# Sums of activation blocks in buffers of the hidden tiles: a feed-forward with more conventional and fewer seven-product sets

## The chip, the cores and the metric

The program runs on one core of a Trainium2 chip, in one launch. The metric is the device time of that launch in microseconds (us), shown as the median of several runs with their lowest and highest. One further run was taken with the hardware profiler; every row below is from that one. Engines are called as the profile calls them: PE is TensorE, DVE is VectorE, ACT is ScalarE, SP is the engine that issues the DMAs here.

## The reference

One inference step of a small diffusion model with two layers. Each layer is a feed-forward, a mixer (attention and pooling) and a second feed-forward; the change touches only the feed-forwards, of which there are four in all. All data are fp32.

```
D_MODEL = 1024
SEQ = 128            # context tokens
DEC_SEQ = 512        # latent tokens
D_FF = ((8 * D_MODEL // 3 + 255) // 256) * 256     # 2816
...
def modulate(h, shift, scale):
    return h * (1 + scale) + shift
...
def ffn_sub(x, g, shift, scale, gate, w_in, w_out):
    h = modulate(rms_norm(x, g), shift, scale)
    a, b = jnp.split(h @ w_in, 2, axis=-1)
    return x + gate * (FFN_RESIDUAL * ((jax.nn.silu(a) * b) @ w_out))
```

The shift, scale and gate come from a product of the conditioning vector with `w_mod`; the kernel computes most of them beside the feed-forwards, as reductions on DVE.

## The kernel before

The 512 latent and 128 context tokens stand together as 640 columns, in two groups of G = 320. The activation is kept transposed: eight k-tiles of 128 rows (channels) by 640 columns. Every fp32 product is made of three fp32r matmuls: an operand is split in a high part (ACT, a copy with rounding) and a low part (DVE, the difference), and the matmuls are high by high, high by low and low by high. `split_w` (L103, L104) does that for a weight unit of 128 by 1024 and `norm_apply` (L295 to L299) for the normalised, modulated activation h; its parts are `hhi` and `hlo`.

The inner width 2816 is 22 f-tiles of 128 rows. An f-tile needs two weight units, one for a and one for b. There are two ways to make one:

- conventional (`in_one`, `start4`, the three units of `start_first`): for each of the two units, 8 k-tiles x 2 groups x 3 = 48 matmuls of 320 columns, 96 for the f-tile;
- a seven-product set (`product_set`): the 2 x 2 block products (two halves of the k-tiles by two token groups, by a and b) are made with seven block products of 4 k-tiles x 3 = 12 matmuls, 84 for the f-tile. It needs sums and differences of the weight blocks (L427 to L432, each on 128 x 512) and of the activation's four blocks h11, h12 (k-tiles 0 to 3 of groups 0 and 1), h21 and h22 (k-tiles 4 to 7).

`combine_h` makes the sums of activation blocks once in each feed-forward. For each k of 0 to 3 it recomputes h in full precision in four temporaries (`h_full`, L396 on DVE and L398 on ACT; group 1 in two pieces, of 192 and 128 columns, because the latent and the context tokens have their own modulation), takes four differences (L407 to L410), and splits each into a high part (ACT) and a low part (DVE L418): `Th`, `Tl` for T1 to T3, and for T4 the parts of h itself, k-tiles 0 to 3 of group 1, which no later product reads otherwise.

A feed-forward starts with f-tiles 0 and 1 (`start4`: four units at once, or in the first feed-forward `start_first`), makes f-tile 2 conventionally (NCONV = 3), and the other 19 as seven-product sets. `hidden` or `hidden7` make silu(a) * b, split it in `hidh`, `hidl` (a pool of 7 buffers each). The output products take the f-tiles in chunks of 6, 6, 5 and 5. `filler` puts the reductions of `w_mod` between (L157, two for each 128 x 1024 tile of it). While `start4` runs, `self.pend` applies the norm to group 1 (`norm_out`).

What sets the order: the program's calls are put on each engine by a scheduler, which can move an instruction past others on its engine; an engine then takes its instructions in the order that results. Pools set more: weight tiles as loaded have 4 buffers (`raw`, shared with the `w_mod` tiles; all loads go through SP), split weights have 5 (`whi`, `wlo`), PSUM has 8 banks. A tile waits until the earlier one in its buffer has been read for the last time.

Of the kernel before, what the change touches and what calls it, by code (L numbers as in the profile page):

```python
# [6 lines left out]
F32 = mybir.dt.float32  # L7
F32R = mybir.dt.float32r
BF16 = mybir.dt.bfloat16
AF = mybir.ActivationFunctionType  # L10
ALU = mybir.AluOpType
# [4 lines left out]
P, D, KT = 128, 1024, 8  # L16
NT, G = 640, 320
NFT = 22
CHUNKS = (6, 6, 5, 5)
NCONV = 3  # L20
EPS = 1e-6
WINDOWS = (2, 4, 8, 16)
NWM = 12
# [8 lines left out]
def grp(a, g):  # L32
    return a[:, g * G:(g + 1) * G]
# [7 lines left out]
class Body:  # L41
    def __init__(self, nc, tc, ctx, i, o):
        self.nc, self.tc, self.i, self.o = nc, tc, i, o
        self.n = 0
        self.pend, self.hold, self.chains = None, None, []
        k = self.keep = self.pool(ctx, "keep", 1)
        self.raw = self.pool(ctx, "raw", 4)
        self.wr = self.pool(ctx, "wr", 5)
        self.hp = self.pool(ctx, "hp", 1)
        self.tp = self.pool(ctx, "tp", 5)  # L50
        self.x = [k.tile([P, NT], F32, name=f"x{m}") for m in range(KT)]
        self.mod = k.tile([P, 2, 2, 9, KT], F32, name="mod")
        self.acol = k.tile([P, 2, 2, 3, KT], F32, name="acol")
        self.bmod = k.tile([P, 2, 9, KT], F32, name="bmod")
        self.gn = k.tile([P, 7, KT], F32, name="gn")
        self.cst = k.tile([P, 640], F32, name="cst")
        self.anti = self.cst[:, 512:640]
        self.ident = self.cst[:, 0:128]
        self.bones = self.cst[:, 128:256]
        self.sel = self.cst[:, 256:352]  # L60
        self.edge = self.cst[:, 352:380]
        self.ones = self.cst[:, 384:512]
# [259 lines left out]
    def norm_out(self, g, nxt):  # L322
        rstd = self.ys[g] = self.rstd(g)
        for m in range(KT):
            self.norm_one(m, g, rstd, nxt)

    def norm_one(self, m, g, rstd, nxt):
        if nxt is None:
# [58 lines left out]
        return p4  # L387


    def h_full(self, m, g, l, s):  # L390

        nc = self.nc
        t = self.g()
        x, y = grp(self.x[m], g), self.ys[g]
        for q, c in PIECES[g]:
            nc.vector.scalar_tensor_tensor(out=t[:, c], in0=x[:, c], scalar=self.acol[:, q, l, s, m:m + 1],  # L396
                                           in1=y[:, c], op0=ALU.mult, op1=ALU.mult)
            nc.scalar.activation(t[:, c], t[:, c], AF.Identity, bias=self.mod[:, q, l, 3 * s, m:m + 1])  # L398
        return t

    def combine_h(self, pool, l, s):

        nc = self.nc
        T = self.T = [[None] * 4 for _ in range(4)]
        for k in range(4):
            h11, h12, h21, h22 = (self.h_full(m, g, l, s) for m in (k, k + 4) for g in range(2))
            nc.vector.tensor_tensor(h11, h12, h11, op=ALU.subtract)  # L407
            nc.vector.tensor_tensor(h12, h22, h12, op=ALU.subtract)
            nc.vector.tensor_tensor(h22, h22, h11, op=ALU.subtract)
            nc.vector.tensor_tensor(h21, h21, h22, op=ALU.subtract)  # L410
            for j, t in enumerate((h11, h22, h12, h21)):
                if j < 3:
                    hi = pool.tile([P, G], F32R, tag=f"Th{j}{k}", name=self.nm("Th"))
                    lo = pool.tile([P, G], F32R, tag=f"Tl{j}{k}", name=self.nm("Tl"))
                else:
                    hi, lo = self.h(k, 1)
                nc.scalar.activation(hi, t, AF.Copy)
                nc.vector.tensor_tensor(lo, t, hi.bitcast(F32), op=ALU.subtract)  # L418
                T[j][k] = hi, lo

    def product_set(self, srcs):

# [11 lines left out]
        w3 = self.split_w(b)  # L434
        T1, T2, T3, T4 = self.T
        h1, h2, h3 = ([self.h(k, g) for k in r] for r, g in ((range(4), 0), (range(4, 8), 0), (range(4, 8), 1)))
# [23 lines left out]
    def ffn(self, ctx, l, j, nxt, fill=(), first=False):  # L460

        nc = self.nc
        fill = list(fill)
        spread = max(0, len(fill) - (32 if first else 28))
        if first:
            with ExitStack() as cs:
                p3 = self.start_first(self.pool(cs, "st", 1))
        hp = self.pool(ctx, "hid", 7)
        Tp = self.pool(ctx, "T", 1)
        win, wout = self.i["w_in"], self.i["w_out"]  # L470
        v = 2 + 6 * j

        def hidden(pa, pb):
            sl = self.t()
            for g in range(2):
                self.last_silu = nc.scalar.activation(grp(sl, g), pa[g][:, :G], AF.Silu)
                if self.last_rs:
                    self.after(self.last_silu, self.last_rs)
                    self.last_rs = None
                nc.vector.tensor_tensor(grp(sl, g), grp(sl, g), pb[g][:, :G], op=ALU.mult)  # L480
            return hid_split(sl)

        def hid_split(sl):
            hi = hp.tile([P, NT], F32R, tag="hidh", name=self.nm("hidh"))
            lo = hp.tile([P, NT], F32R, tag="hidl", name=self.nm("hidl"))
            nc.scalar.activation(hi, sl, AF.Copy)
            nc.vector.tensor_tensor(lo, sl, hi.bitcast(F32), op=ALU.subtract)
            return hi, lo
# [11 lines left out]
        def filler(n):  # L500
            for _ in range(n):
                if fill:
                    self.mod_tile(*fill.pop(0))

        def fill_set(f):

            if f < 7:
                filler(1)
            else:
                filler((f - 6) * spread // 15 - (f - 7) * spread // 15)  # L510

        def in_one(f, ab):
            w, p = self.unit(win[l, j, f, ab]), [self.bank() for _ in range(2)]
            for k in range(KT):
                self.mm3([p[g][:, :G] for g in range(2)], w, k, [self.h(k, g) for g in range(2)], k == 0, k == KT - 1)
            return p

        if first:
            hid = [hidden(p3[0], p3[1])]
            hid.append(hidden(p3[2], in_one(1, 1)))  # L520
        else:
            p4 = self.start4([win[l, j, f, ab] for f in range(2) for ab in range(2)])
            hid = [hidden(p4[0], p4[1]), hidden(p4[2], p4[3])]
        if fill:
            self.mod_load()
        while len(hid) < NCONV:
            pa = in_one(len(hid), 0)
            hid.append(hidden(pa, in_one(len(hid), 1)))
            if first:
                filler(4)  # L530
        self.combine_h(Tp, l, 2 * j)

        def inproj(f):
            hid.append(hidden7(*self.product_set([win[l, j, f, ab] for ab in range(2)])))
# [864 lines left out]
def layout(a):  # L1399
    import numpy as np  # L1400
    C = np.ascontiguousarray
    d = dict(consts())
    xp, xs = a["x_prompt"][0].T, a["x_sample"][0].T[:, tok()]
    d["xT"] = np.concatenate([xs, xp], 1).reshape(KT, P, NT)
# [23 lines left out]
    d["w_pool"] = a["w_pool"][0]  # L1428
    d["pscale"] = C(a["pool_scale"][0].reshape(4, P).T)
    ck = a["cache_nb_k"][0, 0].transpose(1, 2, 0)  # L1430
# [18 lines left out]
def unlay(r):  # L1449
    import numpy as np  # L1450
    y = r["yT"].reshape(D, NT)
    yp = y[:, 512:].T[None]
    ys = np.empty((512, D), y.dtype)
# [21 lines left out]
```

## Time and profile before

| | us |
|---|---|
| median of 3 runs (lowest to highest) | 2393.68 (2390.45 to 2394.62) |
| the profiled execution | 2392.37 |
| its span, first to last instruction | 2390.6 |
| PE busy | 2299.9 (96%) |
| DVE busy | 1949.5 (82%) |
| ACT busy | 1159.0 (48%) |

Busy times overlap. Matmuls are pipelined and a waiting one can still be counted as busy, so the work that PE gets done in a stretch is better read from the number of matmuls in it. [...] In a timeline the duration of an instruction overlaps the start of the next one on its engine, so the time that an instruction takes up on its engine is the distance of the starts.

### The profile page before, as it was taken

Reading aid. Unit: us, or ns where it says so; the run is one execution under the profiler, and the core shown is the slowest. Engines: PE = TensorE matmul, PEld = TensorE weight load, DVE = VectorE, ACT = ScalarE, POOL = GpSimd, SP = SyncE. Lnnn points to the kernel's source line nnn. Section 1 sums busy time; section 2 is a strip of 40 time slices with the busy share of each in tenths; the row PEclk is TensorE's granted clock in tenths of the full one; section 3 lists DMA queues with packets and bytes.
Section 4 is the critical chain, followed back from the end, with each engine's and each line's share of the span. In section 5 each row is a group of like instructions: output and inputs, shape, how many; then the busy total and the mean of one; then the engine's idle time right before and its main releaser. Section 6 shows DMA issues by size and latency. Waiting matters only on the chain.

```text
span 2390.6 us, 40708 instructions
## 1 busy us (share of the span) xinstructions
PE 2299.9 (96%) x15852; PEld 2224.0 (93%) x15852; DVE 1949.5 (82%) x3975; ACT 1159.0 (48%) x2164; POOL 2.2 (0%) x10
## 2 busy tenths in 40 slices
PE   7799999999999999999999999998999999999998
PEld 5799999998888999999989999998888898999997
DVE  6998989785889977786899898969778899565665
ACT  5534343463666534334563425347756665252443
POOL 0000000000000000000000000000000000000000
PEclk9899999999999999999989999999999999999999
DMA  7254535322111433352225353432110013222221
GB/s 288 98 177 135 176 126 180 119 97 86 55 46 46 138 129 123 113 167 75 86 71 186 112 187 124 155 105 79 36 36 28 28 54 104 88 79 84 88 67 67
DMA packets 81088, 253.38 MB, mean 106 GB/s; under 512 B 9600, under 2 KB 15360, under 8 KB 80896
## 3 DMA queue, kind: packets, MB, share of 16 engines
q1 hardware_dynamic: 80896, 250.79, 32.1%
q8 instruction: 125, 2.05, 0.3%
q14 instruction: 67, 0.55, 0.1%
HBM read 247.34 MB, written 3.41 MB: 105 GB/s over the span
## 4 chain that ended last, share of the span: by engine, by line
PE 83%; DVE 11%; ACT 3%; issue 2%; DMA 1%; DVEq 0%; ACTq 0%; SPq 0%
PE mm L124 36%; PE mm L132 13%; PE mm L133 13%; PE mm L135 13%; PE tr L618 2%; PE pv L1251 2%; DVE wlo L104 1%; PE sc L1216 1%; DVE junk L157 1%; DVE g L295 1%; DVE hlo L299 1%; DVE g L396 1%; ACT whi L103 1%; PE pv L1018 1%; PE sc L991 0%
## 5 line engine op out<-in xcount | busy, mean ns | idle before, releaser
L103 ACT ACTIVATE whi<-raw 128x1024 fp32r<-128x1024 f32 (+2 forms) x424 | 411.7, 978 | 553.2 <-PE mm L133 245.4
L104 DVE TENSOR_TENSOR wlo<-raw,whi 128x1024 fp32r<-128x1024 f32 (+2 forms) x424 | 472.1, 1118 | 110.0 <-ACT whi L103 109.6
L132 PE MATMUL mm<-hidh,whi 128*128 128x320 f32 x1408 | 427.4, 310 | 0.0
L133 PE MATMUL mm<-hidl,whi 128*128 128x320 f32 x1408 | 425.7, 308 | 0.0
L124 PE MATMUL mm<-hhi,wlo 128*128 128x320 f32 x1216 | 378.3, 311 | 5.6 <-DVE wlo L104 5.6
L124 PE MATMUL mm<-hhi,whi 128*128 128x320 f32 x1216 | 378.5, 311 | 0.8 <-ACT mm L440 0.8
L124 PE MATMUL mm<-hlo,whi 128*128 128x320 f32 x1216 | 377.5, 310 | 0.0
L135 PE MATMUL mm<-hidh,wlo 128*128 128x320 f32 x1408 | 346.1, 309 | 0.0
L157 DVE CUSTOM_DVE_ANT_0 junk<-rawm,sil 128x1024 bf16<-128x1024 f32 x256 | 311.9, 1218 | 18.1 <-DMA rawm<-in_wmT 14.5
L348 DVE SCALAR_TENSOR_TENSOR x<-mm,mod,x 128x192 f32<-128x192 f32 (+2 forms) x576 | 226.4, 433 | 111.8 <-PE mm L135 110.7
L133 PEld LDWEIGHTS mm<-hidl,whi 128*128 128x128 f32 x1408 | 264.3, 188 | 0.8
L132 PEld LDWEIGHTS mm<-hidh,whi 128*128 128x128 f32 x1408 | 264.3, 188 | 0.8
L135 PEld LDWEIGHTS mm<-hidh,wlo 128*128 128x128 f32 x1408 | 241.4, 188 | 0.0
L124 PEld LDWEIGHTS mm<-hhi,wlo 128*128 128x128 f32 x1216 | 230.6, 190 | 6.0 <-DVE wlo L104 6.0
L132 PE MATMUL mm<-hhi,whi 128*128 128x320 f32 x736 | 228.5, 324 | 7.4 <-ACT hhi L298 7.3
L124 PEld LDWEIGHTS mm<-hhi,whi 128*128 128x128 f32 x1216 | 230.7, 190 | 1.2 <-ACT mm L440 1.2
L124 PEld LDWEIGHTS mm<-hlo,whi 128*128 128x128 f32 x1216 | 230.7, 190 | 0.0
L133 PE MATMUL mm<-hlo,whi 128*128 128x320 f32 x736 | 227.1, 314 | 0.5 <-DVE hlo L299 0.2
L135 PE MATMUL mm<-hhi,wlo 128*128 128x320 f32 x736 | 211.6, 311 | 0.7 <-DVE wlo L104 0.5
L124 PE MATMUL mm<-Th,whi 128*128 128x320 f32 x608 | 192.9, 317 | 8.4 <-ACT whi L103 5.1
L124 PE MATMUL mm<-Tl,whi 128*128 128x320 f32 x608 | 191.2, 314 | 0.0
L124 PE MATMUL mm<-Th,wlo 128*128 128x320 f32 x608 | 190.8, 314 | 0.4 <-DVE wlo L104 0.4
(212 smaller groups left out, 4144.8 us busy)
## 6 DMA issues: line engine op xcount, KB each, us to landing
raw<-in_w_in SPq DMA_DIRECT2D x176, 512.0 KB, 3.5
rawm<-in_wmT SPq DMA_DIRECT2D x128, 512.0 KB, 3.5
raw<-in_w_out SPq DMA_DIRECT2D x64, 384.0 KB, 3.6
raw<-in_w_out SPq DMA_DIRECT2D x64, 320.0 KB, 2.9
wm<-in_wm SPq DMA_DIRECT2D x16, 512.0 KB, 10.2
raw<-in_w_ab SPq DMA_DIRECT2D x12, 512.0 KB, 4.3
raw<-in_w_c SPq DMA_DIRECT2D x10, 512.0 KB, 3.5
sil<-in_c SPq DMA_DIRECT2D x8, 512.0 KB, 5.3
```

What stands on the lines that cost most here:

```text
L103: a = (nc.scalar.activation(hi[:, :n], r[:, :n], AF.Copy), nc.vector.tensor_tensor(lo[:, :n], r[:, :n], hi[:, :n].bitcast(F32), op=ALU.sub ...
L104: nc.vector.tensor_tensor(lo[:, :n], r[:, :n], hi[:, :n].bitcast(F32), op=ALU.subtract))
L124: nc.tensor.matmul(out, a[:, c], b, start=start and first, stop=last, skip_group_check=True)
L132: nc.tensor.matmul(out, hi[:, c], rh, start=start, stop=False)
L133: nc.tensor.matmul(out, hi[:, c], rl, start=False, stop=False)
L135: nc.tensor.matmul(out, lo[:, c], rh, start=False, stop=stop)
L157: nc.vector.tensor_tensor_reduce(out=self.junk, in0=r, in1=self.sil[:, q], op0=ALU.mult, op1=ALU.add, scale=1.0, scalar=0.0, accum_out=sel ...
L295: nc.vector.scalar_tensor_tensor(out=t[:, c], in0=x[:, c], scalar=self.acol[:, q, l, s, m:m + 1], in1=rstd[:, c], op0=ALU.mult, op1=ALU.mult)
L299: nc.vector.scalar_tensor_tensor(out=lo[:, c], in0=t[:, c], scalar=b, in1=hi[:, c].bitcast(F32), op0=ALU.add, op1=ALU.subtract)
L348: nc.vector.scalar_tensor_tensor(out=x[:, c], in0=ps[:, c], scalar=self.mod[:, q, l, v, m:m + 1], in1=x[:, c], op0=ALU.mult, op1=ALU.add)
L618: self.nc.tensor.transpose(ps[:, a * P:(a + 1) * P], src[:, b * P:(b + 1) * P], self.ident)
L1251: nc.tensor.matmul(st["pv"][64 * f:64 * f + 64, ti * P:(ti + 1) * P], V[:, (4, 0, 1, 2, 3)[a], vc], rhs, start=a == 0, stop=a == 4)
```

## The change

- NCONV becomes a number for each feed-forward: 5, 4, 4, 4 conventional f-tiles. The seven-product sets become 17, 18, 18, 18.
- The recomputed h lies in four tiles `hf` of 128 x (4 k-tiles x 320), taken from the pool of the hidden tiles (7 buffers, whose `hidh` and `hidl` are now one tile of 2 x 640).
- The four differences (L443, L447, L448, L452 of the changed kernel) and the splits of T1 to T3 (L430, L431) work on 128 x 1280, one instruction where there were four. T4 is still split by k-tile (L436, L437).
- In the second to fourth feed-forward the norm of group 1 is applied through `apply_full`: it writes h to `hf` (L398 on DVE, L400 on ACT) and splits it from there (L412 on ACT, L413 on DVE), and `combine_h` recomputes group 0 alone.
- `combine_h` is called before the third f-tile, and the splits of T4 (`over()`) stand behind the last conventional product.
- In the first feed-forward the eight `w_mod` tiles near the switch stand in two fours behind the fourth and the fifth f-tile. In the others the four tiles are spread over three sets where they were over four.

```diff
-NCONV = 3
+NCONV = (5, 4, 4, 4)
...
     def norm_out(self, g, nxt):
         rstd = self.ys[g] = self.rstd(g)
         for m in range(KT):
-            self.norm_one(m, g, rstd, nxt)
+            if self.hf and g == 1 and nxt is not None:
+                self.apply_full(m, *nxt)
+            else:
+                self.norm_one(m, g, rstd, nxt)
...
-    def h_full(self, m, g, l, s):
-
-        nc = self.nc
-        t = self.g()
+    def h_full(self, t, m, g, l, s):
+
...
-    def combine_h(self, pool, l, s):
...
+    def h_blocks(self, pool):
+
+        self.hf = [[pool.tile([P, 4, G], F32, tag="hid", name=self.nm("hf")) for _ in range(2)] for _ in range(2)]
+
+    def apply_full(self, m, l, s):
+
+        nc = self.nc
+        t = self.h_full(self.hf[m // 4][1][:, m % 4], m, 1, l, s)
+        hi, lo = self.h(m, 1)
+        self.last_hi = nc.scalar.activation(hi, t, AF.Copy)
+        nc.vector.tensor_tensor(lo, t, hi.bitcast(F32), op=ALU.subtract)
+
+    def combine_h(self, pool, l, s, all_groups):
+
+        nc = self.nc
+        (h11, h12), (h21, h22) = self.hf
+        T = self.T = [None] * 4
+
+        def full(r, gs):
+            for k in range(4):
+                for g in gs:
+                    self.h_full(self.hf[r][g][:, k], 4 * r + k, g, l, s)
+
+        def parts(j, t):
+            if j < 3:
+                hi = pool.tile([P, 4, G], F32R, tag=f"Th{j}", name=self.nm("Th"))
+                lo = pool.tile([P, 4, G], F32R, tag=f"Tl{j}", name=self.nm("Tl"))
                 nc.scalar.activation(hi, t, AF.Copy)
                 nc.vector.tensor_tensor(lo, t, hi.bitcast(F32), op=ALU.subtract)
-                T[j][k] = hi, lo
+                T[j] = [(hi[:, k], lo[:, k]) for k in range(4)]
+                return
+            T[j] = [self.h(k, 1) for k in range(4)]
+            for k, (hi, lo) in enumerate(T[j]):
+                nc.scalar.activation(hi, t[:, k], AF.Copy)
+                nc.vector.tensor_tensor(lo, t[:, k], hi.bitcast(F32), op=ALU.subtract)
+
+        if all_groups:
+            full(0, (0, 1))
+        else:
+            full(0, (0,))
+        nc.vector.tensor_tensor(h11, h12, h11, op=ALU.subtract)
+        parts(0, h11)
+        if all_groups:
+            full(1, (1,))
+        nc.vector.tensor_tensor(h12, h22, h12, op=ALU.subtract)
+        nc.vector.tensor_tensor(h22, h22, h11, op=ALU.subtract)
+        parts(1, h22)
+        parts(2, h12)
+        full(1, (0,))
+        nc.vector.tensor_tensor(h21, h21, h22, op=ALU.subtract)
+        return lambda: parts(3, h21)
...
         fill = list(fill)
+        nconv = NCONV[2 * l + j]
+        early = 8 - 4 * (nconv - 3) if first else 4
...
         def hid_split(sl):
-            hi = hp.tile([P, NT], F32R, tag="hidh", name=self.nm("hidh"))
-            lo = hp.tile([P, NT], F32R, tag="hidl", name=self.nm("hidl"))
+            hid = hp.tile([P, 2, NT], F32R, tag="hid", name=self.nm("hid"))
+            hi, lo = hid[:, 0], hid[:, 1]
             nc.scalar.activation(hi, sl, AF.Copy)
             nc.vector.tensor_tensor(lo, sl, hi.bitcast(F32), op=ALU.subtract)
             return hi, lo
...
         def fill_set(f):
 
             if f < 7:
-                filler(1)
+                filler((f + 1 - nconv) * early // (7 - nconv) - (f - nconv) * early // (7 - nconv))
             else:
...
         else:
+            self.h_blocks(hp)
             p4 = self.start4([win[l, j, f, ab] for f in range(2) for ab in range(2)])
             hid = [hidden(p4[0], p4[1]), hidden(p4[2], p4[3])]
         if fill:
             self.mod_load()
-        while len(hid) < NCONV:
+        if first:
+            self.h_blocks(hp)
+        while len(hid) < nconv:
+            if len(hid) == 2:
+                over = self.combine_h(Tp, l, 2 * j, first)
+                self.hf = None
             pa = in_one(len(hid), 0)
             hid.append(hidden(pa, in_one(len(hid), 1)))
-            if first:
+            if first and len(hid) > 3:
                 filler(4)
-        self.combine_h(Tp, l, 2 * j)
+        over()
```

The tile names in the following rows carry a number for each allocation; `mm` is a PSUM bank, `x`, `acol` and `t` (as a last operand of L396 or L398) are the inputs of h. All are from the second feed-forward, whose first matmul comes at about 725 us, but for the last, from the first.

DVE before, around the end of `combine_h`: its last k (k = 3) and, between its pieces, the low part of a weight unit of the first seven-product set.

```order
L396 SCALAR_TENSOR_TENSOR g_8534<-x_77,acol,t_7881 128x320
L396 SCALAR_TENSOR_TENSOR g_8537<-x_77,acol,t_7881 128x192
L396 SCALAR_TENSOR_TENSOR g_8537<-x_77,acol,t_7881 128x128
L407 TENSOR_TENSOR g_8526<-g_8529,g_8526 128x320
L104 TENSOR_TENSOR wlo_8582<-raw_8562,whi_8581 128x1024
L408 TENSOR_TENSOR g_8529<-g_8537,g_8529 128x320
L418 TENSOR_TENSOR Tl_8547<-g_8526,Th_8546 128x320
L409 TENSOR_TENSOR g_8537<-g_8537,g_8526 128x320
```

DVE of the changed kernel, from the low part of T1 to the low part of the first unit of the first seven-product set (`wlo_8482`). `wlo_8350` and `wlo_8406` belong to the two units of the added f-tile, `mm_8289` and `mm_8290` are the b product of the f-tile before it.

```order
L431 TENSOR_TENSOR Tl_8205<-hf_7893,Th_8204 128x1280
L448 TENSOR_TENSOR hf_7896<-hf_7896,hf_7893 128x1280
L431 TENSOR_TENSOR Tl_8215<-hf_7894,Th_8214 128x1280
L431 TENSOR_TENSOR Tl_8211<-hf_7896,Th_8210 128x1280
L452 TENSOR_TENSOR hf_7895<-hf_7895,hf_7896 128x1280
L516 TENSOR_TENSOR t_8339<-t_8339,mm_8289 128x320
L516 TENSOR_TENSOR t_8339<-t_8339,mm_8290 128x320
L104 TENSOR_TENSOR wlo_8350<-raw_8347,whi_8349 128x1024
L523 TENSOR_TENSOR hid_8344<-t_8339,hid_8344 128x640
L104 TENSOR_TENSOR wlo_8406<-raw_8403,whi_8405 128x1024
L461 TENSOR_TENSOR s_1361_8479<-raw_8477 128x512
L104 TENSOR_TENSOR wlo_8482<-raw_8475,whi_8481 128x1024
```

The differences now stand together ahead of the split of the added f-tile's first unit, and this split stands behind the multiplication by the product before it (L516); the weights of the first seven-product set come behind them all.

PE before, from the end of the b product of f-tile 2 into the first seven-product set.

```order
L135 MATMUL mm_8365<-hhi_7906,wlo_8362 128x320
L135 MATMUL mm_8366<-hhi_7906,wlo_8362 128x320
L124 MATMUL mm_8585<-hhi_7899,whi_8566 128x320
L124 MATMUL mm_8585<-hlo_7907,whi_8566 128x320
L124 MATMUL mm_8585<-hhi_7899,wlo_8567 128x320
```

PE of the changed kernel, from the end of the same product (now `mm_8289`, `mm_8290`) into the added f-tile.

```order
L135 MATMUL mm_8289<-hhi_7804,wlo_8286 128x320
L135 MATMUL mm_8290<-hhi_7804,wlo_8286 128x320
L132 MATMUL mm_8353<-hhi_7797,whi_8349 128x320
L133 MATMUL mm_8353<-hlo_7805,whi_8349 128x320
L132 MATMUL mm_8354<-hhi_7797,whi_8349 128x320
L133 MATMUL mm_8354<-hlo_7805,whi_8349 128x320
L132 MATMUL mm_8409<-hhi_7797,whi_8405 128x320
L133 MATMUL mm_8409<-hlo_7805,whi_8405 128x320
L132 MATMUL mm_8410<-hhi_7797,whi_8405 128x320
L133 MATMUL mm_8410<-hlo_7805,whi_8405 128x320
L124 MATMUL mm_8500<-hhi_7797,whi_8481 128x320
L124 MATMUL mm_8500<-hlo_7805,whi_8481 128x320
L135 MATMUL mm_8353<-hhi_7797,wlo_8350 128x320
```

Ten matmuls that need only high parts of weights, six of them from later products, stand ahead of the first one that reads `wlo_8350`.

DVE of the changed kernel in the first feed-forward, from the multiplication by the b product of the fourth f-tile (`mm_939`, `mm_940`) to the low part of the fifth f-tile's first unit (`wlo_1016`). The ISA rows are the reductions of L157.

```order
L516 TENSOR_TENSOR t_989<-t_989,mm_939 128x320
L516 TENSOR_TENSOR t_989<-t_989,mm_940 128x320
L157 ISA junk,mod<-rawm_1005,sil 128x1024
L157 ISA mod 128x1
L523 TENSOR_TENSOR hid_994<-t_989,hid_994 128x640
L157 ISA junk,mod<-rawm_1009,sil 128x1024
L157 ISA mod 128x1
L104 TENSOR_TENSOR wlo_1016<-raw_1013,whi_1015 128x1024
```

Here too the split of the next unit stands behind a multiplication that reads the product just finished, and behind reductions.

## Rows read from the trace of the kernel before

**Rows 1.** The page: the span, the busy times, and the span in 40 slices of 59.8 us with the busy share of PE and the granted clock, in tenths.

```profile
span 2390.6 us, 40708 instructions
PE 2299.9 (96%) x15852; PEld 2224.0 (93%) x15852; DVE 1949.5 (82%) x3975; ACT 1159.0 (48%) x2164; POOL 2.2 (0%) x10
PE   7799999999999999999999999998999999999998
PEclk9899999999999999999989999999999999999999
```

**Rows 2.** PE in stretches: us, their length, PE's busy time with the number of matmuls, granted clock, busy share of the DMA engines, GB/s. The first four begin where the four feed-forwards go from conventional f-tiles to the seven-product sets, the fifth is inside the second feed-forward.

```profile
77.00:117.00 40.00, 24.93 (x137) 0.79 0.25 82
769.00:809.00 40.00, 34.13 (x197) 0.87 0.24 79
1213.00:1253.00 40.00, 34.39 (x188) 0.83 0.23 76
1976.00:2016.00 40.00, 34.07 (x196) 0.87 0.25 79
800.00:840.00 40.00, 40.00 (x275) 1.00 0.54 172
```

**Rows 3.** DVE in the same four stretches; the same columns, with DVE's busy time and instructions.

```profile
77.00:117.00 40.00, 39.52 (x77) 0.79 0.25 82
769.00:809.00 40.00, 36.89 (x70) 0.87 0.24 79
1213.00:1253.00 40.00, 35.51 (x69) 0.83 0.23 76
1976.00:2016.00 40.00, 36.73 (x70) 0.87 0.25 79
```

**Rows 4.** The waits of PE: engine, line, for whom, us in total, times, longest.

```profile
PE mm L124 <- ACT Th L417: 14.0, 6, 2.6
PE mm L124 <- DVE wlo L104: 6.0, 2, 5.6
```

**Rows 5.** The first matmul of the first seven-product set, in the first and the second feed-forward, from the timeline of PE: start, duration, instruction.

```profile
77.86 0.31 PE L124 MATMUL mm<-hhi,whi 128*128 128x320 f32 x1
770.24 0.31 PE L124 MATMUL mm<-hhi,whi 128*128 128x320 f32 x1
```

**Rows 6.** The timeline of DVE in the second feed-forward: start, duration, line, instruction, how many. Rows that follow on each other give what an instruction takes up.

```profile
754.24 0.48 DVE L410 TENSOR_TENSOR g<-g,g 128x320 f32<-128x320 f32 x1
754.64 0.48 DVE L418 TENSOR_TENSOR Tl<-g,Th 128x320 fp32r<-128x320 f32 x1
755.05 1.14 DVE L396 SCALAR_TENSOR_TENSOR g<-x,acol,t 128x320 f32<-128x320 f32 x3
756.10 1.22 DVE L104 TENSOR_TENSOR wlo<-raw,whi 128x1024 fp32r<-128x1024 f32 x1
757.24 0.88 DVE L480 TENSOR_TENSOR t<-t,mm 128x320 f32<-128x320 f32 x2
758.03 0.54 DVE L396 SCALAR_TENSOR_TENSOR g<-x,acol,t 128x320 f32<-128x320 f32 x1
758.50 0.68 DVE L114 TENSOR_TENSOR slo<-s,shi 128x512 fp32r<-128x512 f32 x1
759.10 1.55 DVE L487 TENSOR_TENSOR hidl<-t,hidh 128x640 fp32r<-128x640 f32 x2
760.57 0.68 DVE L430 TENSOR_TENSOR raw<-raw,raw 128x512 f32<-128x512 f32 x1
761.17 0.48 DVE L407 TENSOR_TENSOR g<-g,g 128x320 f32<-128x320 f32 x1
761.58 1.21 DVE L157 CUSTOM_DVE_ANT_0 junk<-rawm,sil 128x1024 bf16<-128x1024 f32 x1
762.72 0.08 DVE L157 DVE_READ_ACCUMULATOR2_ANT mod<- 128x1 f32 x1
```

**Rows 7.** The timeline of ACT at the same place; in brackets the idle time ahead of the instruction and what ended it.

```profile
754.89 1.06 ACT L103 ACTIVATE whi<-raw 128x1024 fp32r<-128x1024 f32 x1 [0.40 <-PE mm L133]
755.86 0.75 ACT L476 ACTIVATE t<-mm 128x320 f32<-128x320 f32 x2
756.49 1.92 ACT L150 ACTIVATE sil<-sil 128x2048 f32<-128x2048 f32 x1
758.29 1.36 ACT L486 ACTIVATE hidh<-t 128x640 fp32r<-128x640 f32 x2
763.25 0.77 ACT L476 ACTIVATE t<-mm 128x320 f32<-128x320 f32 x2 [0.75 <-PE mm L135]
```

**Rows 8.** DVE in the first feed-forward, from its timeline, at the first reductions.

```profile
57.60 0.88 DVE L480 TENSOR_TENSOR t<-t,mm 128x320 f32<-128x320 f32 x2 [0.53 <-ACT t L476]
60.39 1.23 DVE L157 CUSTOM_DVE_ANT_0 junk<-rawm,sil 128x1024 bf16<-128x1024 f32 x1 [1.90 <-ACT sil L150]
```

**Rows 9.** The page's list of DMA issues: the loads of the units of the conventional and seven-product f-tiles; how many, KB each, median us from issue to landing.

```profile
raw<-in_w_in SPq DMA_DIRECT2D x176, 512.0 KB, 3.5
```

**Rows 10.** PE in three stretches of 4 us in the first feed-forward; columns as in rows 2.

```profile
96.00:100.00 4.00, 0.00 (x0) 0.69 0.00 0
100.00:104.00 4.00, 3.44 (x11) 0.50 0.65 199
104.00:108.00 4.00, 3.49 (x22) 0.96 0.56 195
```

**Rows 11.** DVE inside `combine_h` of the second feed-forward, where it waits for ACT.

```profile
781.75 0.49 DVE L407 TENSOR_TENSOR g<-g,g 128x320 f32<-128x320 f32 x1 [1.19 <-ACT g L398]
```

More of the change, by code (lines that the diff above doesn't have):

```diff
@@ L44, in __init__ @@
         self.n = 0
-        self.pend, self.hold, self.chains = None, None, []
+        self.pend, self.hold, self.chains, self.hf = None, None, [], None
         k = self.keep = self.pool(ctx, "keep", 1)
@@ L399, in h_full @@
         return t
-    def combine_h(self, pool, l, s):
+    def h_blocks(self, pool):
+        self.hf = [[pool.tile([P, 4, G], F32, tag="hid", name=self.nm("hf")) for _ in range(2)] for _ in range(2)]
+    def apply_full(self, m, l, s):
         nc = self.nc
[L404 to L416, printed above, removed]
+        t = self.h_full(self.hf[m // 4][1][:, m % 4], m, 1, l, s)
+        hi, lo = self.h(m, 1)
+        self.last_hi = nc.scalar.activation(hi, t, AF.Copy)
+        nc.vector.tensor_tensor(lo, t, hi.bitcast(F32), op=ALU.subtract)
```

## The prediction

> **What bounds the kernel now.** I read the slices of the page first [rows 1]: PE is busy nearly everywhere, and PEclk leaves 9 in a few slices only. Busy time hides a waiting PE, so I counted matmuls. In dense work 275 of them fit in 40 us [rows 2], as the fifth row has it, 0.1455 us each. F1 to F4 are the four feed-forwards. Where each goes over to the seven-product sets, the same 40 us hold 137, 197, 188 and 196 [rows 2]: 138, 78, 87 and 79 too few, together 382 x 0.1455 = 55.6 us of PE time lost, 20.1 of it in F1 and 11.3, 12.7 and 11.5 in the others. [...] DVE is busy for 35.5 to 39.5 of the 40 us [rows 3], and PE waits for the parts of T and for low parts of weights [rows 4]. Cause: f-tile 2 ends at 77.9 in F1 and at 770.2 in F2 [rows 5], when `combine_h` is still on DVE; the first set needs T1 to T3 whole and split weights that stand between the pieces of `combine_h`. These four places are DVE-bound, the rest of a feed-forward is PE-bound.
>
> **The change part by part.** *Added on PE.* Five f-tiles (2 + 1 + 1 + 1) go from 84 to 96 matmuls: 60 x 0.1455 = 8.7 us, on the path, since PE bounds there.
>
> *The old loss goes.* The sums now run beside one f-tile more (two more in F1) of conventional work, 14.0 us of PE each (96 x 0.1455). -55.6 us. What is late next decides the rest.
>
> *Prices on DVE*, from the distances of starts [rows 6]: a difference or split of 320 columns 0.40, of 512 0.60, of 640 0.74, of 1024 1.14; h for 320 columns in one piece 0.47, in two pieces 1.05 - 0.47 = 0.58; a pair of L480 0.8; a reduction 1.14. No row is 1280 wide. Between 320 and 1024 a column costs (1.14 - 0.40) / 704 = 1.05 ns, so 1.14 + 256 x 1.05 ns = 1.4 us. The bounds are 1.14 (no dearer than 1024) and 4 x 0.40 = 1.6 (four of 320). I take 1.4, the line through the nearest rows; over 28 of them the ends are -7 and +6 us.
>
> *F2 to F4, the next wait.* Before its sums DVE has to split the second unit of f-tile 2 (`wlo_8286`), and its buffer comes free only when `start4` has read its first unit for the last time: the same unit's high part waits for PE until 754.9 today [rows 7]. By then DVE has done all that stands ahead of it in the new order; so everything after it counts from 754.9, however much cheaper `apply_full` is. High part 1.0, to 755.9; `wlo_8286` 1.14, to 757.0; a pair of L516 0.8, to 757.8; one h piece; then L523 waits for ACT, which has sil (1.92) ahead of it [rows 7], to 759.0; two L523 1.5, to 760.5. Then seven h pieces at 0.47 (3.3), seven wide operations (9.8), a pair of L516 (0.8) and `wlo_8350` (1.14): 775.5. PE finishes the first product of f-tile 2 at 763.2 [rows 7] and, 48 x 0.1455 = 7.0 later, the second at 770.2. It has ten matmuls (1.5 us) that need no `wlo_8350`, and then stands from 771.7 to 775.5: 3.8 us. Behind it, `wlo_8406` and the first set's `wlo_8482` are split some 2 and 3.6 us later, long before PE, 13 us later, wants the latter; the sums are all done. So 3.8 us each in F2, F3 and F4 (their old losses lie within 1.4 us of each other, and the order of DVE is the same): +11.4. At the least, with sums that cost nothing, L516 alone must wait for 770.2, and 0.8 + 1.14 leave 0.4 us.
>
> *F1.* Here L516 and the reductions sit ahead of `wlo_1016`, the fifth f-tile's first unit. DVE from 60.4, where the first reduction starts today [rows 8]: 7 reductions 8.0, four weight splits 4.6, three pairs of L516 2.4, four L523 3.0, h 8 x 0.47 + 8 x 0.58 = 8.4, seven wide operations 9.8, sum 36.2: 96.6, with 0.9 for hand-overs such as L523 behind sil 97.5. PE is through the fourth f-tile at 77.9 + 14.0 = 91.9; eight matmuls can go ahead (1.2): 4.4 us lost. (The load of that unit waits on SP for the buffer of the first w_mod tile, whose second reduction ends 8.4 us ahead of `wlo_1016`, at 89.1; it lands 3.5 later [rows 9], its high part is there at 93.6, so the load hides behind DVE.) PE then has 88 matmuls of the fifth f-tile, to 110.3. DVE has nine reductions, one split and three parts of T4 (12.6), to 110.1, and must still do a pair of L516 for that f-tile, a few small adds of the modulation, taken at 0.5, a part of T4, L461, L523 and the first set's first weight split: 0.8 + 0.5 + 0.4 + 0.6 + 0.74 + 1.14 = 4.2, so 114.5; PE has four matmuls (0.6) meanwhile: 3.6 lost. The set's second split follows 0.60 x 6 + 1.14 later, when PE is just there: 0.3. Together 8.3 us.
>
> *The clock.* An idle PE also pays afterwards. Between 96 and 100 no matmul runs, the clock falls, and from 100 to 104 it is 0.50, with 11 matmuls where 27 would fit [rows 10]; it is whole again soon after 104, so some 4 us at half rate, 2.1 us lost after an idle of 5. I forecast five waits of 3.6 to 4.4 us. Bounds: nothing, if the idle is too short, or 2.1 each. I take 1.5, nearer to the row: +7.5. [...]
>
> *Hidden.* `apply_full` brings the first part of group 1 about 0.5 us later, but PE asks for it over 2 us after DVE starts it; no cost. DVE and ACT have less work afterwards (each f-tile made conventionally saves DVE four operations of 512 and more), and PE is dense there anyway: no gain. The w_mod tiles are the same in number.
>
> *Sum*, on the profiled execution: span 2390.6 - 55.6 + 8.7 + 11.4 + 8.3 + 7.5 = 2370.9; the execution lies 1.8 us above its span, 2372.7; the median of the runs shown is 1.3 above that execution: **2374.0**.
>
> **Rivals.**
> 1. *No wait is left.* If DVE came to the added weights in time, only the 8.7 would remain: 2393.7 - 55.6 + 8.7 = 2347. For it: DVE has idle time before 754.9. Against it: a split behind a multiplication that reads the product just finished cannot be ready when that product ends. [...] Chance 0.09.
> 2. *Coarse steps come late.* T1 was ready in its first quarter after 0.40 us and now after 1.4; if a product waited for each of the three T this way, 3 x 1.0 x 4 = 12 us more: 2386. Against it: the first set starts 13 us after the last sum. [...] Chance 0.06.
> 3. *Hand-overs between ACT and DVE.* Each wide sum goes DVE, ACT, DVE; one hand-over costs 1.2 us of idle DVE today [rows 11]. With four such in each feed-forward on the way to the added weights: 16 x 1.2 = 19, 2393, no change. Against it: the new order puts other work between most of them. Chance 0.08.
> 4. *Slower: the wide operations cost more than their width.* Seven lie in each feed-forward ahead of the added f-tile's weights, so any excess goes through PE's wait in full. The gain of 19.7 is eaten at 19.7 / 28 = 0.7 us each, at 2.1 us; at double price, 2.8, the time is 2374 + 28 x 1.4 = 2413. For it: no row shows this width. Against it: four widths lie on one line [rows 6]. Chance 0.07.
>
> **How the numbers follow.** The forecast holds 0.70, with a range of its own from 2364 (clock holds) to 2386. The unknown prices (-7, -7.5; +6, +3) and rivals 2 and 3 widen it to 2359 to 2390. A measurement of this kernel tells 0.2% (4.8 us) from no change: faster is the forecast, 1 and 2, 0.85; same is 3, 0.08; slower is 4, 0.07.
>
> **What would show it.** The same 40 us windows from the first set's start should hold about 260 matmuls or more, and DVE's wide operations take about 1.4 us each. PE's longest waits in F2 to F4 should be for L104's low parts at the start of the added f-tile, some 3.8 us, no longer for `Th`; in F1 two waits, at the fifth f-tile and at the first set. PEclk should dip after each. I am wrong if PE waits for `Th` or `Tl` as long as now, if the wide operations take 2 us, or if PE runs through the added f-tile without a pause.

## The result, and the profile after

The changed kernel takes 2376.5 us (median of 4 runs, 2373.75 to 2379.49) where the kernel before takes 2394.2 (4 runs on the same chip): a ratio of 0.993, 95% interval 0.991 to 0.995. The forecast was 2374.0, with 2359 to 2390 as its range. The profiled execution took 2375.2.

The page:

```profile
span 2373.4 us, 40480 instructions
PE 2297.9 (97%) x15912; PEld 2227.2 (94%) x15912; DVE 1900.9 (80%) x3779; ACT 1124.8 (47%) x2074; POOL 2.2 (0%) x10
```

The waits of PE (engine, line, for whom, us in total, times, longest):

```profile
PE mm L135 <- DVE wlo L104: 12.7, 5, 3.9
PE mm L132 <- ACT whi L103: 2.6, 2, 1.8
PE mm L124 <- ACT shi L113: 2.5, 1, 2.5
```

Against [rows 1], PE has 60 matmuls more and a span 17.2 us shorter. The waits tell why. Those for `Th` [rows 4] are gone; in their place stands the low part of a weight, read by L135, which is a conventional product and no longer a set.

PE in stretches of 40 us (busy time, matmuls, granted clock, with 1.00 for the full one; 275 fit):

```profile
80.00:120.00 40.00, 33.80 (x205) 0.92 0.40 132
120.00:160.00 40.00, 39.49 (x269) 1.00 0.55 176
760.00:800.00 40.00, 36.10 (x236) 0.96 0.32 105
1200.00:1240.00 40.00, 36.09 (x236) 0.96 0.33 106
1960.00:2000.00 40.00, 36.09 (x229) 0.91 0.32 106
```

They hold 70, 6, 39, 39 and 46 too few, together 200 x 0.1455 = 29.1 us, where [rows 2] lacked 55.6. With the 8.7 us of added products that makes -55.6 + 8.7 + 29.1 = -17.8, and the span fell by 17.2: the account closes.

By stage it closes to about 1 us. R is the moment at which ACT may overwrite the buffer that `start4` has read. Its rows in F2, F3 and F4, after the change and then before it (F2 before is in [rows 7]):

```profile
750.39 1.06 ACT L103 ACTIVATE whi<-raw 128x1024 fp32r<-128x1024 f32 x1 [6.53 <-PE mm L133]
1190.48 1.06 ACT L103 ACTIVATE whi<-raw 128x1024 fp32r<-128x1024 f32 x1 [6.67 <-PE mm L133]
1947.11 1.06 ACT L103 ACTIVATE whi<-raw 128x1024 fp32r<-128x1024 f32 x1 [6.53 <-PE mm L133]
```

```profile
1199.01 1.06 ACT L103 ACTIVATE whi<-raw 128x1024 fp32r<-128x1024 f32 x1 [0.59 <-PE mm L133]
1961.65 1.06 ACT L103 ACTIVATE whi<-raw 128x1024 fp32r<-128x1024 f32 x1 [0.39 <-PE mm L133]
```

R is 4.5, 8.5 and 14.5 us earlier, the end 17.2: F1 with the first mixer gave 4.5, F2 4.0, F3 with the second mixer 6.0 and F4 2.7 (by the counts of matmuls 5.5, 3.9, 5.3 and 3.1). ACT and DVE now idle ahead of R (6.5 us on ACT), where the kernel before had pieces of `combine_h` [rows 6]; this time is not used.

DVE in F2 from R on (start, duration, line, instruction, how many; in brackets idle time ahead):

```profile
751.49 1.23 DVE L104 TENSOR_TENSOR wlo<-raw,whi 128x1024 fp32r<-128x1024 f32 x1 [7.06 <-ACT whi L103]
...
754.56 1.56 DVE L523 TENSOR_TENSOR hid<-t,hid 128x640 fp32r<-128x640 f32 x2 [0.59 <-ACT hid L522]
756.04 2.86 DVE L398 SCALAR_TENSOR_TENSOR hf<-x,acol,t 128x320 f32<-128x320 f32 x6
758.89 1.49 DVE L443 TENSOR_TENSOR hf<-hf,hf 128x1280 f32<-128x1280 f32 x1
760.30 0.55 DVE L398 SCALAR_TENSOR_TENSOR hf<-x,acol,t 128x320 f32<-128x320 f32 x1
760.77 1.49 DVE L447 TENSOR_TENSOR hf<-hf,hf 128x1280 f32<-128x1280 f32 x1
762.17 1.48 DVE L431 TENSOR_TENSOR Tl<-hf,Th 128x1280 fp32r<-128x1280 f32 x1
...
767.80 1.48 DVE L452 TENSOR_TENSOR hf<-hf,hf 128x1280 f32<-128x1280 f32 x1
769.21 0.88 DVE L516 TENSOR_TENSOR t<-t,mm 128x320 f32<-128x320 f32 x2
770.00 1.22 DVE L104 TENSOR_TENSOR wlo<-raw,whi 128x1024 fp32r<-128x1024 f32 x1
```

From one start to the next a wide operation takes 1.41 us (758.89 to 760.30). From 751.49 on the timeline marks one gap, of 0.59; the split that PE wants, `wlo_8350`, is the last row and is done at 771.1, R + 20.8. PE has stood for it, from 767.4 to 771.27. The clock is still whole when the matmuls begin again and falls 0.8 us later:

```profile
771.50:772.00 0.50, 0.50 (x5) 1.00 0.00 0
772.00:772.50 0.50, 0.50 (x4) 0.58 0.80 115
773.00:777.00 4.00, 4.00 (x21) 0.69 0.62 219
```

### The profile page after: what moved, and what is told of

Its sections match the earlier page's. It is cut to its first block, busy times and chain, and to the rows that moved or that the text cites. A ratio compares the mean times of both kernels' runs of the same rounds, so it can differ in the third digit from the quotient of the medians.

```text
span 2373.4 us, 40480 instructions
## 1 busy us (share of the span) xinstructions
PE 2297.9 (97%) x15912; PEld 2227.2 (94%) x15912; DVE 1900.9 (80%) x3779; ACT 1124.8 (47%) x2074; POOL 2.2 (0%) x10
## 4 chain that ended last, share of the span: by engine, by line
PE 87%; DVE 9%; ACT 3%; issue 1%; DMA 1%; DVEq 0%; SPq 0%; ACTq 0%
PE mm L124 34%; PE mm L135 15%; PE mm L132 15%; PE mm L133 14%; PE tr L660 2%; PE pv L1293 2%; PE sc L1258 1%; DVE wlo L104 1%; DVE junk L157 1%; PE pv L1060 1%; ACT whi L103 0%; DVE Tl L431 0%; PE mm L810 0%; PE mm L809 0%; PE mm L808 0%
## 5 line engine op out<-in xcount | busy, mean ns | idle before, releaser
L132 PE MATMUL mm<-hid,whi 128*128 128x320 f32 x1408 | 427.1, 310 | 0.0
L133 PE MATMUL mm<-hid,whi 128*128 128x320 f32 x1408 | 425.7, 308 | 0.0
L124 PE MATMUL mm<-hhi,wlo 128*128 128x320 f32 x1136 | 351.5, 309 | 0.4 <-DVE wlo L104 0.4
L124 PE MATMUL mm<-hhi,whi 128*128 128x320 f32 x1136 | 351.3, 309 | 0.0
L124 PE MATMUL mm<-hlo,whi 128*128 128x320 f32 x1136 | 350.8, 309 | 0.0
L135 PE MATMUL mm<-hid,wlo 128*128 128x320 f32 x1408 | 346.1, 308 | 0.0
L157 DVE CUSTOM_DVE_ANT_0 junk<-rawm,sil 128x1024 bf16<-128x1024 f32 x256 | 312.0, 1219 | 16.4 <-DMA rawm<-in_wmT 14.4
L132 PE MATMUL mm<-hhi,whi 128*128 128x320 f32 x896 | 280.3, 325 | 9.5 <-ACT hhi L298 6.8
L133 PE MATMUL mm<-hlo,whi 128*128 128x320 f32 x896 | 279.8, 318 | 0.5 <-DVE hlo L299 0.3
L133 PEld LDWEIGHTS mm<-hid,whi 128*128 128x128 f32 x1408 | 264.3, 188 | 0.8
L132 PEld LDWEIGHTS mm<-hid,whi 128*128 128x128 f32 x1408 | 264.3, 188 | 0.8
L135 PE MATMUL mm<-hhi,wlo 128*128 128x320 f32 x896 | 251.9, 316 | 12.9 <-DVE wlo L104 12.7
L135 PEld LDWEIGHTS mm<-hid,wlo 128*128 128x128 f32 x1408 | 241.6, 188 | 0.0
L124 PEld LDWEIGHTS mm<-hhi,wlo 128*128 128x128 f32 x1136 | 213.6, 188 | 0.8 <-DVE wlo L104 0.8
L124 PEld LDWEIGHTS mm<-hlo,whi 128*128 128x128 f32 x1136 | 213.7, 188 | 0.0
L124 PEld LDWEIGHTS mm<-hhi,whi 128*128 128x128 f32 x1136 | 213.7, 188 | 0.0
L132 PEld LDWEIGHTS mm<-hhi,whi 128*128 128x128 f32 x896 | 170.8, 193 | 19.7 <-ACT hhi L298 10.0
L135 PEld LDWEIGHTS mm<-hhi,wlo 128*128 128x128 f32 x896 | 165.1, 193 | 15.8 <-DVE wlo L104 14.9
L133 PEld LDWEIGHTS mm<-hlo,whi 128*128 128x128 f32 x896 | 173.3, 194 | 4.9 <-DVE hlo L299 2.6
```

What stands on the lines that cost most here:

```text
L124: nc.tensor.matmul(out, a[:, c], b, start=start and first, stop=last, skip_group_check=True)
L132: nc.tensor.matmul(out, hi[:, c], rh, start=start, stop=False)
L133: nc.tensor.matmul(out, hi[:, c], rl, start=False, stop=False)
L135: nc.tensor.matmul(out, lo[:, c], rh, start=False, stop=stop)
L157: nc.vector.tensor_tensor_reduce(out=self.junk, in0=r, in1=self.sil[:, q], op0=ALU.mult, op1=ALU.add, scale=1.0, scalar=0.0, accum_out=sel ...
```

## The experiments

Nine kernels were run, with the kernel before on the same chips; its median there lay between 2392.9 and 2394.1 us, so that the 2376.5 us of the changed kernel, from another chip, can be set beside theirs to about 1 us. Theory: the gain needs sums that run beside conventional work instead of in front of the first set, and what is left of the loss is DVE's queue between R and the added f-tile's first split. The rivals stand in each expectation.

**Products alone.** `more_products_only` is the kernel before with

```diff
-NCONV = 3
+NCONV = (5, 4, 4, 4)
```

> The kernel before with 5, 4, 4 and 4 conventional f-tiles and nothing else; combine_h stays as it was, behind the last of them, and the w_mod fillers are placed as in the changed kernel. Theory (the sums must be able to run beside the products; the added products alone give nothing): the fourth part of each step overwrites h of group 1, which every conventional product reads, and its four temporaries are held till then, so the sums still come after the last of them; the old loss of 55.6 us stays and 60 matmuls x 0.1455 = 8.7 us are added: 2403, between 2398 and 2407. Rival (the added products alone hide the sums): as the changed kernel, 2376.

Measured: 2394.5 us (11 runs) against 2393.2, ratio 1.0004 (0.9996 to 1.0013). No gain, so the rival falls, but it is also 3.5 us below the theory's range. PE waits for T as before:

```profile
PE mm L124 <- ACT Th L417: 16.9, 13, 2.7
```

The part that was off is F1. The same stretch of F1 (78 to 106 us), DVE's w_mod reductions (L157) alone, in the kernel before and then in this one (each reduction leaves two records):

```profile
78.00:106.00 28.00, 2.44 (x4) 0.70 0.15 48
```

```profile
78.00:106.00 28.00, 13.22 (x22) 1.00 0.46 151
```

With two more f-tiles of products 11 reductions run beside them, where there were 2, at a clock of 1.00 instead of 0.70; they still stand between the first pieces of `combine_h`, but PE does not wait for these now. Between 80 and 160 us PE makes 459 matmuls instead of 423, 36 x 0.1455 = 5.2 us won, which pays part of the 8.7.

**Sums alone.** `sums_only` is the changed kernel with the following (by the formula for `early` all eight w_mod tiles of F1 then stand beside the sets):

```diff
-NCONV = (5, 4, 4, 4)
+NCONV = (3, 3, 3, 3)
```

> The changed kernel with 3 conventional f-tiles in all four feed-forwards: the sums stand before the third, four k-tiles at a time, and no products are added. Theory (both parts are needed): in F2 to F4 the sums run beside f-tile 2, but the first set's first split stands behind L516, the last sum and the four parts of T4 on DVE and is ready some 5 us after PE is through, its third split 3 us later; with the clock some 10 us lost each against 11.3 to 12.7 before; in F1 about 17 against 20. Sum 2394.2 - 3 x 2 - 3 = 2385, between 2379 and 2391. Rival A (the order of the sums alone is the gain): 2368 to 2377. Rival B (without added products nothing is gained): 2392 or more. PE's longest waits should be at the first set, for wlo of L104.

Measured: 2389.3 us (11 runs), ratio 0.9984 (0.9975 to 0.9993): a gain of 4 us, inside the theory's range and in neither rival's. Its waits:

```profile
PE mm L124 <- DVE wlo L104: 20.8, 5, 6.6
PE mm L124 <- ACT whi L103: 8.3, 1, 8.3
```

The wait is for weights, as in the changed kernel, but at the first set, and longer. The longest, 8.3 us, is for a high part, in F1, where the expectation had named low parts. So the two halves give -4 and +1 us alone and -18 together.

**h made again.** `h_made_again` drops `apply_full`:

```diff
-            if self.hf and g == 1 and nxt is not None:
-                self.apply_full(m, *nxt)
-            else:
-                self.norm_one(m, g, rstd, nxt)
+            self.norm_one(m, g, rstd, nxt)
...
-                over = self.combine_h(Tp, l, 2 * j, first)
+                over = self.combine_h(Tp, l, 2 * j, True)
```

> The changed kernel without apply_full: norm_one makes h of group 1 as before, and combine_h makes its eight k-tiles again for the sums, as in F1, in F2 to F4 too. Theory (DVE from the release of the weight buffer to the added f-tile's first split is one queue that PE waits for in full): eight pieces of 0.58 us are added to it and one wide operation of 1.41 falls behind L516, so PE waits 3.2 us longer in each of F2 to F4, 9.7 us, and 0 to 2 us more for the clock each: 2376.5 + 13 = 2389, between 2385 and 2394. Rival (the queue has slack, the wait is set by something else): 2376 to 2379.

Measured: 2394.9 us (11 runs), ratio 1.0002 (0.9993 to 1.0011): the whole gain is gone, 1 us more than the range allowed. PE's wait:

```profile
PE mm L135 <- DVE wlo L104: 26.3, 4, 8.6
PE mm L124 <- ACT whi L103: 1.8, 3, 0.6
```

The end of DVE's queue in F2:

```profile
774.78 0.88 DVE L513 TENSOR_TENSOR t<-t,mm 128x320 f32<-128x320 f32 x2
775.58 1.48 DVE L449 TENSOR_TENSOR hf<-hf,hf 128x1280 f32<-128x1280 f32 x1
776.98 0.82 DVE L520 TENSOR_TENSOR hid<-t,hid 128x640 fp32r<-128x640 f32 x1
777.71 2.35 DVE L104 TENSOR_TENSOR wlo<-raw,whi 128x1024 fp32r<-128x1024 f32 x2
```

The queue has no slack, as the theory has it; the wait grows from 3.9 to 8.6, with another 0.6 for a high part just ahead of it. The size was off because the last wide operation (L449) did fall behind the multiplication (L513) but stayed ahead of the split, so nothing was saved, and L520, which stands behind the split in the changed kernel, stands ahead of it here.

**Narrow steps.** `narrow_steps` makes the wide operations in four:

```diff
+        def sub(o, a, b):
+            for k in range(4):
+                nc.vector.tensor_tensor(o[:, k], a[:, k], b[:, k], op=ALU.subtract)
...
-        nc.vector.tensor_tensor(h11, h12, h11, op=ALU.subtract)
+        sub(h11, h12, h11)
```

and so on for the other sums and for the high and low parts of T1 to T3.

> The changed kernel with each operation of 1280 columns of combine_h made as four of 320, on DVE and on ACT, in the same buffers; no work is left out. Theory (DVE's queue up to the added f-tile's split is paid in full): seven times 4 x 0.40 instead of 1.41, 1.3 us in each feed-forward, 5 in all: 2381.5, between 2378 and 2385. Rival (coarse steps come late, rival 2 of the prediction): finer steps let DVE and ACT start earlier and the time falls to 2373 or less.

Measured: 2382.5 us (6 runs), ratio 0.9955 (0.9943 to 0.9967), 6 us above the changed kernel. PE's wait is 5.5 at the longest, and eight narrow operations take 3.2 us (764.91 to 768.13) where two wide ones take 2.8:

```profile
PE mm L135 <- DVE wlo L104: 16.7, 4, 5.5
```

```profile
764.91 3.30 DVE L442 TENSOR_TENSOR hf<-hf,hf 128x320 f32<-128x320 f32 x8
768.13 3.30 DVE L432 TENSOR_TENSOR Tl<-hf,Th 128x320 fp32r<-128x320 f32 x8
```

In F2 that makes PE's wait 1.6 us longer, priced at 1.3. R in F2 is 4.0 us later than in the changed kernel, so F1 with the first mixer has 4.0 of the 8.2 us between the two profiled executions:

```profile
754.38 1.06 ACT L103 ACTIVATE whi<-raw 128x1024 fp32r<-128x1024 f32 x1 [6.53 <-PE mm L133]
```

Rival 2 of the prediction (coarse steps) is refuted here with the opposite sign.

**Weights first.** `weights_first` moves the added f-tile's first unit ahead of the sums, and each later unit one place ahead:

```diff
+        def ahead(n):
+            while todo and len(ready) < n:
+                ready.append(self.unit(win[(l, j) + todo.pop(0)]))
...
+                ahead(3)
                 over = self.combine_h(Tp, l, 2 * j, first)
```

> The changed kernel with the unit of the fourth f-tile loaded and split before combine_h, and each later unit of the conventional f-tiles before the multiplication of the f-tile ahead of it; no work is added or left out. Theory (PE waits in F2 to F4 because wlo of that unit stands on DVE behind the sums and L516): the waits of 3.9 us and the half clock after them go, 39, 39 and 46 matmuls x 0.1455 = 18 us in F2 to F4; in F1 the wait at the fifth f-tile (some 5 us with the clock) goes, the one at the first set may grow by 2. 2376.5 - 18 - 3 = 2355, between 2351 and 2361. Rival (PE waits there for the sums, for a PSUM buffer or for the load, whatever the order on DVE): 2372 or more, with the wait as long and on another tile.

Measured: 2358.4 us (4 runs), ratio 0.986 (0.985 to 0.988), within the range, and the rival falls. Of L135's waits for `wlo` 0.5 us is left. PE in F2, in the same 40 us, then in F1:

```profile
760.00:800.00 40.00, 39.51 (x270) 1.00 0.28 93
80.00:120.00 40.00, 33.73 (x212) 0.91 0.40 132
120.00:160.00 40.00, 38.93 (x263) 1.00 0.58 189
```

DVE's two splits there, the second now ahead of the sums:

```profile
749.79 1.23 DVE L104 TENSOR_TENSOR wlo<-raw,whi 128x1024 fp32r<-128x1024 f32 x1 [7.07 <-ACT whi L103]
...
754.44 1.23 DVE L104 TENSOR_TENSOR wlo<-raw,whi 128x1024 fp32r<-128x1024 f32 x1
755.58 2.86 DVE L398 SCALAR_TENSOR_TENSOR hf<-x,acol,t 128x320 f32<-128x320 f32 x6
```

The sums are not faster; in F2 to F4 PE no longer waits behind them, and the clock stays at 1.00 (in the 40 us from 1200 and from 1960 too, with 270 and 269 matmuls). The same edit moves the loads of these units ahead too. In F2 to F4 they can't be what PE had stood for: in the changed kernel it multiplied with the high part of the same unit just before it stood for the low part. F1 gained next to nothing, 475 matmuls in these 80 us against 474 in the changed kernel: the wait at the fifth f-tile went, but the one at the first set grew by over 3 us, where the expectation allowed 2.

**Narrow steps with the weights first** (`weights_first_narrow`, both edits).

> The kernel with the added weights ahead of the sums, with each operation of 1280 columns made as four of 320. Theory (with no PE wait behind the sums their width no longer matters): 2358, between 2355 and 2361. Rival (the wide form gains by itself, wherever the sums stand): 5 us slower, 2362 or more.

Measured: 2366.2 us (4 runs), ratio 0.9888 (0.9875 to 0.9902): the theory fell, by 8 us, and the rival holds. The width still matters with the weights ahead. R in F2, first with the wide operations, then with the narrow:

```profile
748.69 1.06 ACT L103 ACTIVATE whi<-raw 128x1024 fp32r<-128x1024 f32 x1 [6.53 <-PE mm L133]
752.90 1.06 ACT L103 ACTIVATE whi<-raw 128x1024 fp32r<-128x1024 f32 x1 [6.53 <-PE mm L133]
```

F1 with the first mixer loses 4.2 of the 9.0 us between the two profiled executions. In F1 a queue on DVE still stood in front of PE, at the first set, which the expectation had passed over. The rest is spread over the other stages, 1 to 2 us each; what exactly it is stays open.

**Four in F1.** `four_in_first` is the changed kernel with

```diff
-NCONV = (5, 4, 4, 4)
+NCONV = (4, 4, 4, 4)
```

> The changed kernel with 4 conventional f-tiles in the first feed-forward instead of 5 (12 matmuls fewer, 4 of the 8 early w_mod tiles beside the sets); F2 to F4 are unchanged. Theory (the second added f-tile of F1 hides nothing that is not lost again at its own end): one of F1's two waits goes with its clock, 5 to 6 us, and 1.7 us of matmuls; the first set comes behind the same queue on DVE (L516, reductions, the split) that the fifth f-tile came behind, and its third split costs 2 more: 2376.5 - 5 = 2372, between 2366 and 2378. Rival (F1's sums need both added f-tiles): 2382 or more, with PE waiting for Th or Tl.

Measured: 2374.3 us (5 runs), ratio 0.9918 (0.9905 to 0.993); the changed kernel's interval overlaps. The second added f-tile of F1, with four w_mod tiles beside it, buys nothing there, and the rival falls.

**The reductions spread.** `weights_first_spread` takes the kernel with the weights first and changes

```diff
-        early = 8 - 4 * (nconv - 3) if first else 4
+        early = 4
...
-            if first and len(hid) > 3:
+            if first and len(hid) == 4:
                 filler(4)
```

> The kernel with the added weights ahead of the sums, and four of F1's eight early w_mod tiles beside the fifth f-tile moved on beside the sets of f-tiles 5 and 6, two each; no work is left out. Theory (F1's remaining loss, 75 matmuls x 0.1455 = 11 us between 80 and 160, is the first set's split standing behind the w_mod reductions on DVE): most of it goes, 9 us: 2358.4 - 9 = 2349, between 2346 and 2354. Rival (DVE has no room beside the sets, so the wait only moves there): 2356 to 2361.

Measured: 2351.9 us (4 runs), ratio 0.9825 (0.9812 to 0.9838), the fastest of all. F1, between 80 and 120 us:

```profile
80.00:120.00 40.00, 39.63 (x271) 1.00 0.40 132
```

66 matmuls more than in the changed kernel; 21 fewer between 120 and 160, so part of the wait did move to the sets, as the rival has it: 6.4 us were gained of the 9 expected.

**And with four in F1** (`spread_four_in_first`).

> The kernel with the added weights ahead of the sums and four early w_mod tiles beside the sets, with 4 conventional f-tiles in the first feed-forward instead of 5; nothing else differs. Theory (what the fifth f-tile of F1 hides is DVE's queue of reductions and the first set's splits): without it the first set's split stands behind L516 and five reductions, some 8 us after PE is through the fourth f-tile, with 2 to 4 us more for the clock and the third split, and 1.7 us of matmuls are saved: 2352 + 9 = 2361, between 2356 and 2365. Rival (with the weights ahead one added f-tile hides all, as in F2 to F4): 2352 - 1.7 = 2350.

Measured: 2357.6 us (5 runs), ratio 0.9849 (0.9835 to 0.9862): 6 us slower. R in F2, first with five, then with four:

```profile
741.83 1.06 ACT L103 ACTIVATE whi<-raw 128x1024 fp32r<-128x1024 f32 x1 [6.52 <-PE mm L133]
747.60 1.06 ACT L103 ACTIVATE whi<-raw 128x1024 fp32r<-128x1024 f32 x1 [6.53 <-PE mm L133]
```

With the weights first alone R was at 748.69, no better than with four f-tiles here. So the order of the weights by itself does not make the fifth f-tile worth having; it is worth 6 us once four of the eight w_mod tiles have moved on from it. Whether it would be so with the weights still behind the sums was not run.

## Why the prediction was right

The forecast was 2.5 us too low. Its terms hold but for the size of the clock and, in F1, two steps that cost little.

- *Old loss* and *added on PE* (-55.6 and +8.7): the waits for `Th` are gone and 15912 matmuls are there.
- *F2 to F4, the next wait*, 3.8 us each: 3.9 measured. The split was forecast at R + 20.6 (775.5 from 754.9) and ended at R + 20.8. `weights_first` shows the cause: with the split ahead of the sums the wait is gone.
- *F1*, 8.3 us. At the fifth f-tile:

```profile
94.93 0.41 PE L132 MATMUL mm<-hhi,whi 128*128 128x320 f32 x1 [0.85 <-ACT whi L103]
97.55 0.42 PE L132 MATMUL mm<-hhi,whi 128*128 128x320 f32 x1 [1.76 <-ACT whi L103]
99.14 0.56 PE L135 MATMUL mm<-hhi,wlo 128*128 128x320 f32 x2 [0.74 <-DVE wlo L104]
```

  PE stood 3.4 us in three pieces, forecast 4.4. The end of it is the forecast `wlo_1016` (99.0, forecast 97.5), but the load was not hidden: PE first waits for high parts, whose loads came late (ACT starts the two at 93.8 and 96.4). The step "the load hides behind DVE" was wrong, at no price, since the low part came last all the same.

  At the first set:

```profile
116.63 0.58 PE L124 MATMUL mm<-Th,shi 128*128 128x320 f32 x1 [2.50 <-ACT shi L113]
117.84 0.64 PE L124 MATMUL mm<-hhi,wlo 128*128 128x320 f32 x1 [0.36 <-DVE wlo L104]
```

  PE stood 2.9 us, forecast 3.6 and 0.3. The forecast had it wait for the first low part alone; most of the wait was for `shi`, the high part of the sum that L461 makes in the same queue on DVE.
- All waits by the records: 12.7 in the L135 row, and in F1 another 2.6 and 2.5 for high parts and 0.9 in smaller ones, 18.7 us; forecast 11.4 + 8.3 = 19.7.
- *The clock*, +7.5: the mis-sized term. Of the 29.1 us lost, 29.1 - 18.7 = 10.4 are in no wait, 2.1 for each of the five waits, the upper bound of the forecast, which took 1.5. Most of it is the half clock: the clocks of the five stretches of 40 us are together 0.25 short of 1.00, which is 10 us at most, since in F4 the clock fell about a microsecond before the wait was over (it is 0.50 from 1967 on, and the next matmul starts at 1967.99). The rest was not taken apart. The clock fell at each of the five waits: in F1 it is 0.62 from 100 to 104 and 0.50 from 118 to 120, in F2 0.69 in the 4 us from 773, with 21 matmuls where 27 fit, in F3 0.50 from 1213 to 1215 and in F4 0.50 from 1968 to 1970. In F2 the first 0.8 us behind the wait still ran at full clock.
- *Prices on DVE*: a wide operation was taken at 1.4 us and takes 1.41; rival 4 (over 2.1) is refuted by the rows.
- Rival 1 (no wait left, 2347) fell for this kernel, but `weights_first_spread`, at 2352, is close to what it priced. Rival 3 (hand-overs): the queue of F2 has one marked gap, of 0.59 us. Rival 2 (coarse steps): with finer steps `narrow_steps` is 6 us slower.
- *Hidden: `apply_full`* was costed at nothing, which held: PE has no wait for L412 or L413. Only `h_made_again` shows what it is for: 4.6 us of h per feed-forward that would stand behind R, and with it the whole gain.
- Of the signs, the 260 matmuls or more in 40 us from the first set's start came in F2 to F4 (275 from 785) and not in F1 (237 from 113), where the sets wait too.

## What to carry to other kernels

When a stall goes, walk the engine's queue from the last event that it had to wait for (here a buffer coming free) to the first thing that the next consumer needs; if nothing in between can be skipped, each microsecond in it is paid, and the clock adds its part (here waits of 3.9 us in each of F2 to F4, and at most 10 us of clock in all). The first remedy is then the order: the small split that somebody waits for goes ahead of the long work that nobody waits for (18 us here). Speed still counts after it: the narrow operations cost 6 us before and 8 us after the weights had moved ahead. Halves of such a change measured alone can show next to nothing (-4 and +1 us) where both give -18.

## What was not expected

Adding 4.6 us of DVE work per feed-forward in F2 to F4 (`h_made_again`) cost 18 us where 14 were added. L520 ahead of the split accounts for some 2 of the difference. The waits grew by 26.3 - 12.7 = 13.6 for the low parts and 1.8 for high parts, and with them the granted clock fell, in F2 from 0.96 to 0.87 over the same 40 us, with 194 matmuls instead of 236:

```profile
760.00:800.00 40.00, 30.77 (x194) 0.87 0.20 66
```
